# The last two heads of grouped-query attention as one written sequence, with three output groups left open

## The chip, the cores and the metric

The kernel runs on one core of one Trainium2 chip. The metric is device time in microseconds (us) of one launch; lower is better. TensorE is also called PE, VectorE DVE, ScalarE ACT, GpSimd POOL, and SyncE SP; SP issues the DMAs.

## The reference

Two layers of a trunk with two token mixers side by side. 512 latent tokens and 256 context tokens, width 1024, fp32. Each layer, for branch b (grouped-query attention, 8 query heads on 2 key heads, head width 64) and branch a (neighbourhood attention):

```python
px = hx @ w_in                                     # split into queries, keys, values, gate paths, merge gates
b_att = _gqa_latent(qb, k_all, v_all)              # softmax(q k / 8) v over 256 context + 512 latent keys
o_a = (a_att * jax.nn.silu(a_z)) @ w_o_a
o_b = (b_att * jax.nn.silu(b_z)) @ w_o_b
merged = jax.nn.sigmoid(g_a) * o_a + jax.nn.sigmoid(g_b) * o_b
x_new = x + gate_x * (merged @ w_out)
```

In layer 0 the context tokens go through the same steps (their queries read context keys only); in layer 1 only the 512 latent tokens do.

## The kernel before

Every product of fp32 values is made of reduced-precision parts: a value is split into a hi part (a cast on ACT) and a lo part (a subtraction on DVE or POOL), and a product is three matmuls (hi x hi, lo x hi, hi x lo; lines 351 to 353). A scheduler sorts the instructions of each engine by a timeline of its own; where the program calls `in_program_order` or `behind`, the written order is kept on the engines named.

Names that the text uses:

- `psf` is one PSUM bank (its pool has one buffer); `pst` are two banks for transposes; during grouped-query attention `pss` are two tiles of two banks each for scores, `psv` is one bank for values. Afterwards the last five banks are `psx`.
- For a head, `gq_scores` makes four score tiles of 128 queries x 768 keys (`pss`, L718 and L719), the row maximum (`mx`), the exp on ACT (`p`, with its row sum `r`), and `softmax_tail` scales `p` on DVE (blocks 0 and 2) or POOL (blocks 1 and 3, `GQ_POOL`). In layer 0, `ctx_scores` does the same for the context queries.
- `gq_values` goes through six blocks of 128 keys. A block is four transposes of `p` into one `pst` bank (L669), the cast to `pth` on ACT (L672), the rest `ptl` on DVE (L673), and two matmuls into `psv` (L972 with `pth`, L973 with `ptl`). `pth` and `ptl` have two buffers each. After the last block `head_out` adds the two halves of `psv` in `ho` (ACT L681, DVE L682) and multiplies the gate path `zb` with it (POOL L683). In layer 0 a seventh block (`ctx_values`, L746 and L747, 256 columns) does the context queries.
- `zb` is then split into `gbh` (ACT, L557) and `gbl` (POOL, L558), a tile row `f` for each pair of heads: the operands of the product with `w_o_b`.
- `pipeline` runs scores of head h, then values of head h - 1, then some of the `fill` pieces. In this stage these are merge-gate projections and the product of branch a with `w_o_a`: psf groups of 12 matmuls each (`psf<-gah,whi` and the like), of 512 columns and, in layer 0, also of 256 columns for the context. A group is emptied by one DVE instruction (L592, into `tg`), and the next group needs the same bank.
- After attention, `o_chunks("b", ...)` makes the product with `w_o_b`, in groups of 12 matmuls for each of eight column tiles f, with `evac_b` (L1007 to L1011) merging the two branches into `tg` and splitting the sum into `mh` and `ml`, the operands of the product with `w_out`. Weights come by DMA into `raw` and are split into `whi` (ACT, L336) and `wlo` (DVE or POOL, L338).

Of the kernel before, what the change touches and what calls it, by code (L numbers as in the profile page):

```python
# [8 lines left out]
F32 = mybir.dt.float32  # L9
F32R = mybir.dt.float32r  # L10
# [48 lines left out]
def R(ap):  # L59
    return ap.bitcast(F32R)  # L60


def F(ap):
    return ap.bitcast(F32)
# [3 lines left out]
def hybrid_kernel(es: ExitStack, tc, x, ctx, cvec, w_ada, w_ada0, small, gvec, w_in, w_o_a, w_o_b, w_out,  # L68
# [13 lines left out]
    def nm(s):  # L82
        uid[0] += 1
        return f"{s}_{uid[0]}"
# [283 lines left out]
    def chan_proj(w, f, a, n0, n1, evac):  # L368

        ps = psw(n1 - n0)  # L370
        nk = len(w)
        for k in range(nk):
            hi, lo = a(0, k), a(1, k)
            mm3(ps, (w[k][0][:, 128 * f:128 * f + 128], w[k][1][:, 128 * f:128 * f + 128]),
                (R(hi[:, n0:n1]), R(lo[:, n0:n1])), k == 0, k == nk - 1)
        evac(f, n0, n1, ps)

    hp = {"late": [], "lag": 0}

# [110 lines left out]
    def layer(l, hx, nxt, mid):  # L490
# [159 lines left out]
        if True:  # L650
# [22 lines left out]
                V.tensor_tensor(lo[:, n0:n1], pt[:, n0:n1], F(hi[:, n0:n1]), ALU.subtract)  # L673
                return hi, lo

            def head_out(po, e, dst):

                n = dst.shape[-1]
                m, o = 64 * e, 64 * (1 - e)
                t1 = att["p"].tile([128, 512], F32, tag="ho", name=nm("ho"), bufs=1)  # L680
                S.copy(t1[m:m + 64, :n], po[o:o + 64, :n])  # L681
                V.tensor_tensor(t1[m:m + 64, :n], po[m:m + 64, :n], t1[m:m + 64, :n], ALU.add)  # L682
                G.tensor_tensor(dst, dst, t1[m:m + 64, :n], ALU.mult)  # L683

            def rows(a, half):
                return a[64 * half:64 * half + 64]
# [147 lines left out]
                head_out(po, e, zv[64 * e:64 * e + 64, h // 2, 0:512])  # L834
                return vsl

            def pipeline(fill, spread, scores_of, values_of, last=None, bg=[]):

                n = len(fill)
                prev = None  # L840
                for h in range(8):
                    att["bg"] = bg if h > 3 or pm["n"] == 1 else []
                    st = scores_of(h)
# [103 lines left out]
            def gq_scores(q, kh, kl):  # L947
                ps_ = []
                for i in range(4):
                    pss = ps_score(768)  # L950
                    scores(pss, q[:, 128 * i:128 * i + 128], kh, kl,
                           [(0, 512, cut(0, 512)), (512, 256, cut(512, 768))])
                    p = p_tile()
                    mx = sp.tile([128, 2], F32, tag="mx", name=nm("mx"), bufs=8)
                    V.tensor_reduce(mx[:, 0:1], pss, AX, ALU.max, negate=True)
                    r = sp.tile([128, 2], F32, tag="r", name=nm("r"), bufs=8)
                    S.activation(p, pss, AF.Exp, bias=mx[:, 0:1], accum_out=r[:, 0:1])
                    softmax_tail(p, 768, r[:, 0:1], [(0, 768)], G if i in GQ_POOL else None)
                    ps_.append(p)
                    run(att["bg"], 1)  # L960
                return ps_
# [30 lines left out]
            pipeline(fill, 8, gq_first, values_of(zb, gq_values), early, bg)  # L992
            gq_es.close()

        with tc.tile_pool(name=f"mrg{l}", bufs=1, reuse_waits="tile") as mp:
            open_ps(x=5)
            extra = lambda name: mp.tile([128, 3072], F32, tag="extra", name=nm(name))
            gv = mp.tile([128, nv, DM], F32, tag="gate", name=nm("gate"), bufs=1)
            for v in range(nv):
                src = gd[l][8 * v:8 * v + 8].rearrange("k p -> (k p)").unsqueeze(0)  # L1000
                nc.sync.dma_start(gv[:, v, :], src.to_broadcast([128, DM]))
            hilo(zb, gated["b"], [3])
            mg = []

            def evac_b(f, n0, n1, ps):
                a, b = tg_part(0, f, n0, n1), tg_part(1, f, n0, n1)
                V.scalar_tensor_tensor(b, b, 1.0, ps, ALU.add, ALU.mult)  # L1007
                V.tensor_tensor(a, a, b, ALU.add)
                hi, lo = [m[:, f % 4, n0:n1] for m in mg[f // 4]]
                S.copy(R(hi), a)  # L1010
                V.tensor_tensor(R(lo), a, hi, ALU.subtract)  # L1011
            chunks = o_chunks("b", None, evac_b)
            chunks[0][0]()
            for i in range(4):
                if i < 3:
                    chunks[i + 1][0]()
                if i % 2 == 0:
                    mg.append(hilo_tiles("m"))
                for piece in chunks[i][1]:
                    piece()  # L1020
# [219 lines left out]
```

## Time and profile before

| | |
|---|---|
| median of 3 runs | 1148.73 us (1148.03 to 1149.26) |
| profiled execution, time | 1149.07 us |
| profiled execution, span | 1147.0 us |
| granted TensorE clock | 0.999 of full speed |
| layer 0, heads 6 and 7 | about 528 to 562 us from the span's start |
| layer 1, heads 5 to 7 | about 1054 to 1078 us |

The profile is one execution on the chip. A line of the order of time has the start, the duration, the engine, the line of the kernel, the operation with output and input tiles, and the count; in square brackets the idle time of that engine before it and what ended it. The duration of a matmul contains its latency, and matmuls overlap, so what a matmul costs is the distance from its start to the next one's.

### The profile page before, as it was taken

What the parts mean: (1) busy time and instruction counts of PE and PEld (TensorE: products, weight loads), DVE (VectorE), ACT (ScalarE), POOL (GpSimd) and SP (SyncE); (2) the same over time, 40 slices, a digit from 0 to 9 for tenths busy, and PEclk for the clock granted to TensorE, in tenths of its full rate; (3) what the DMA queues carried; (4) which work ended last, traced back from release to release, by engine and by line L of the source; (5) the groups of instructions that cost most, each with busy time, mean ns of one, the idle gap of its engine ahead of it and who ended that gap; (6) DMA issues with size and microseconds to landing.
All of it is one profiled execution on the core that took longest, in us unless ns stands there. A gap on an engine that the chain in (4) does not pass through costs nothing.

```text
span 1147.0 us, 17434 instructions
## 1 busy us (share of the span) xinstructions
PE 1123.5 (98%) x6136; PEld 949.2 (83%) x6136; DVE 818.3 (71%) x1533; ACT 580.3 (51%) x1185; POOL 483.0 (42%) x449
## 2 busy tenths in 40 slices
PE   7999999999999999999999999999999999999998
PEld 5788888888988888888788787888888888887786
DVE  6777688997454786697588755469787665898563
ACT  6553366655433565665330355336666355766421
POOL 1073355453374343453411227345554664465311
PEclk9999999999999999999999999999999999999999
DMA  9645311333322232451434424633332333152143
GB/s 370 232 127 156 90 51 60 105 110 111 106 101 89 95 103 92 92 221 38 149 127 130 151 70 122 193 89 115 97 113 74 111 102 101 65 176 90 61 133 92
DMA packets 89695, 135.08 MB, mean 118 GB/s; under 512 B 10789, under 2 KB 52745, under 8 KB 88969
## 3 DMA queue, kind: packets, MB, share of 16 engines
q1 hardware_dynamic: 89328, 133.87, 36.8%
q8 instruction: 48, 0.79, 0.3%
q14 instruction: 39, 0.31, 0.1%
q10 hardware_dynamic: 280, 0.12, 0.0%
HBM read 116.63 MB, written 17.32 MB: 117 GB/s over the span
## 4 chain that ended last, share of the span: by engine, by line
PE 80%; DVE 7%; DMA 4%; issue 3%; ACT 3%; POOL 2%; SPq 0%; POOLq 0%; ACTq 0%; DVEq 0%
PE psx L353 12%; PE psx L352 12%; PE psx L351 11%; PE psf L351 9%; PE psf L352 9%; PE psf L353 9%; PE pst L669 4%; DMA raw<-in_w_in_dram 2%; PE pss L718 2%; PE pss L719 2%; PE psv L973 2%; PE psv L972 1%; PE pss L795 1%; PE pst L431 1%; DMA rawb<-in_w_ada_dram 1%
## 5 line engine op out<-in xcount | busy, mean ns | idle before, releaser
L673 DVE TENSOR_TENSOR ptl<-pst,pth 128x512 fp32r<-128x512 f32 (+1 forms) x176 | 115.9, 671 | 46.4 <-ACT pth L672 45.4
L672 ACT CAST pth<-pst 128x512 fp32r<-128x512 f32 (+1 forms) x176 | 99.3, 577 | 86.7 <-PE pst L669 55.8
L338 POOL TENSOR_TENSOR wlo<-raw,whi 128x512 fp32r<-128x512 f32 x68 | 95.6, 1409 | 105.1 <-ACT whi L336 83.9
L351 PE MATMUL psf<-hx,whi 128*128 128x512 f32 (+1 forms) x368 | 139.2, 378 | 0.6 <-ACT zt L516 0.6
L352 PE MATMUL psf<-hx,whi 128*128 128x512 f32 (+1 forms) x368 | 138.2, 375 | 0.0
L353 PE MATMUL psf<-hx,wlo 128*128 128x512 f32 (+1 forms) x368 | 137.8, 374 | 0.0
L351 PE MATMUL psx<-whi,hx 128*128 128x512 f32 (+1 forms) x368 | 137.6, 375 | 0.0
L353 PE MATMUL psx<-whi,hx 128*128 128x512 f32 (+1 forms) x368 | 135.9, 369 | 0.1
L352 PE MATMUL psx<-wlo,hx 128*128 128x512 f32 (+1 forms) x368 | 135.7, 369 | 0.0
L336 ACT CAST whi<-raw 128x512 fp32r<-128x512 f32 x136 | 82.7, 621 | 51.6 <-DMA raw<-in_w_in_dram 35.6
L321 ACT CAST whi<-raw 128x512 fp32r<-128x512 f32 x88 | 53.9, 623 | 99.6 <-PE psx L353 38.1
L669 PE MATMUL pst<-ident,p 128*128 128x128 f32 x640 | 99.9, 272 | 1.4 <-DVE ptl L673 0.8
L324 POOL TENSOR_TENSOR wlo<-raw,whi 128x512 fp32r<-128x512 f32 x36 | 50.9, 1416 | 110.0 <-ACT whi L321 74.6
L338 DVE TENSOR_TENSOR wlo<-raw,whi 128x512 fp32r<-128x512 f32 x68 | 68.6, 1010 | 28.1 <-ACT whi L336 27.2
L669 PEld LDWEIGHTS pst<-ident,p 128*128 128x128 f32 x640 | 77.8, 140 | 13.0 <-DVE ptl L673 1.3
L658 POOL TENSOR_SCALAR r<-r 128x1 f32<-128x1 f32 x64 | 22.4, 350 | 152.2 <-DVE r L653 145.2
L659 POOL TENSOR_TENSOR p<-p,r 128x512 f32<-128x512 f32 (+1 forms) x64 | 84.2, 1316 | 5.1
L353 PEld LDWEIGHTS psx<-whi,hx 128*128 128x128 f32 x368 | 69.4, 189 | 12.6 <-DVE hx L1137 1.0
L351 PEld LDWEIGHTS psx<-whi,hx 128*128 128x128 f32 x368 | 69.5, 189 | 12.4 <-issue 0.8
L353 PEld LDWEIGHTS psf<-hx,wlo 128*128 128x128 f32 x368 | 69.4, 188 | 11.8
L351 PEld LDWEIGHTS psf<-hx,whi 128*128 128x128 f32 x368 | 69.4, 189 | 11.4 <-ACT zt L516 0.8
L352 PEld LDWEIGHTS psx<-wlo,hx 128*128 128x128 f32 x368 | 69.5, 189 | 10.8
(252 smaller groups left out, 3056.0 us busy)
## 6 DMA issues: line engine op xcount, KB each, us to landing
raw<-in_w_in_dram SPq DMA_DIRECT2D x168, 256.0 KB, 2.9
rawb<-in_w_ada_dram SPq DMA_DIRECT2D x64, 256.0 KB, 2.9
gs<-zt SPq DMA_DIRECT2D x32, 256.0 KB, 2.1
raw<-in_w_out_dram SPq DMA_DIRECT2D x32, 256.0 KB, 2.9
tg<-gs SPq DMA_DIRECT2D x4, 1536.0 KB, 6.8
rawx<-in_w_ada_dram SPq DMA_DIRECT2D x8, 512.0 KB, 7.9
raw<-in_w_o_a_dram SPq DMA_DIRECT2D x16, 256.0 KB, 2.8
raw<-in_w_o_b_dram SPq DMA_DIRECT2D x16, 256.0 KB, 2.8
```

Source lines behind the costliest of these rows:

```text
L321: S.copy(hi[:, :n], raw[:, :n])
L324: e.tensor_tensor(lo[:, :n], raw[:, :n], F(hi[:, :n]), ALU.subtract)
L336: S.copy(hi, raw)
L338: lo_eng(i).tensor_tensor(lo, raw, F(hi), ALU.subtract)
L351: T.matmul(ps, lhs[0], rhs[0], start=first, stop=False)
L352: T.matmul(ps, lhs[0], rhs[1], start=False, stop=False)
L353: T.matmul(ps, lhs[1], rhs[0], start=False, stop=last)
L659: G.tensor_tensor(p[:, c0:c1], p[:, c0:c1], r[:, i:i + 1].to_broadcast([128, c1 - c0]), ALU.mult)
L669: T.transpose(pt[:, c0:c0 + 128], src, ident)
L672: S.copy(hi[:, n0:n1], pt[:, n0:n1])
L673: V.tensor_tensor(lo[:, n0:n1], pt[:, n0:n1], F(hi[:, n0:n1]), ALU.subtract)
L718: T.matmul(ps[:, c0:c0 + n], q, sl(kh), start=True, stop=False)
```

## The change

From head 7 on, `pipeline` hands over to a `tail`: it first runs all fills that are left, then `gq_tail`. This writes the values of heads 6 and 7 as one sequence of 12 blocks (14 in layer 0, with the two context blocks in the middle), with the order on PE, ACT and DVE fixed. The transposes of a block come three blocks ahead of its matmuls; four banks (the two `pst` and one `pss` tile) and three pairs of hi and lo tiles take turns, the third pair being taken from the weight buffers `whi` and `wlo`. Head 6 collects in `psv`, head 7 in `psf`, the context blocks in the other `pss` tile. The product with `zb` moves from POOL to DVE, and so does the split of the last tile row of `zb` (`gate_part`). Behind the blocks come three column groups of the product with `w_o_b`, each with its first three of four tile rows (9 of 12 matmuls), left open; their last three matmuls follow when the last tile row is split. Their weights are loaded ahead, with the split on POOL. For head 7 the softmax scaling goes to POOL for blocks 0 and 2 in place of 1 and 3.

```diff
             def pipeline(fill, spread, scores_of, values_of, last=None, bg=[], tail=None):
...
                     st = scores_of(h)
+                    if h == 7 and tail is not None:
+                        run(fill, len(fill))
+                        last()
+                        run(bg, len(bg))
+                        return tail(prev, st)
...
-                    softmax_tail(p, 768, r[:, 0:1], [(0, 768)], G if i in GQ_POOL else None)
+                    softmax_tail(p, 768, r[:, 0:1], [(0, 768)], G if i in ((0, 2) if att["h"] == 7 else GQ_POOL) else None)
...
+            lead = [(f, 0, 512) for f in range(3)]
...
+            def gq_tail(st6, st7):
+                need_wb(0, pool_lo)
+                at = len(nc.cur_bb.bb.instructions)
+                before = next(i for i in nc.cur_bb.bb.instructions[::-1] if i.engine == ON_PE)
+                s0, s1 = psw(1024, "s"), psw(1024, "s")
+                banks = [psw(512, "t"), psw(512, "t"), s0[:, 0:512], s0[:, 512:1024]]
...
+                po6, po7 = psw(512, "v"), psw()
...
+                def turn_block(b):
+                    if b < len(blocks):
+                        pt, (hi, lo) = banks[b % 4], parts[b % 3]
+                        for src, c0 in blocks[b][0]:
+                            T.transpose(pt[:, c0:c0 + 128], src, ident)
+                        S.copy(hi, pt)
+                        V.tensor_tensor(lo, pt, F(hi), ALU.subtract)
+                for b in range(3):
+                    turn_block(b)
+                for b, (_, mm, out) in enumerate(blocks):
+                    mm(*parts[b % 3])
+                    turn_block(b + 3)
+                    if out:
+                        out()
+                    if first and b == 9:
+                        gate_part(512, 768)
+                for (f, n0, n1), ps in zip(lead, (po6, s1[:, 0:512], s1[:, 512:1024])):
+                    chan_mm(ps, wb[f // 2], f % 2, act_b, n0, n1, 0, 3)
+                    open_sums.append((f, n0, n1, ps))
+                gate_part(0, 512)
+                in_program_order((ON_PE, ON_ACT, ON_DVE), nc.cur_bb.bb.instructions[at:], {ON_PE: before.name})
+                for f, n0, n1, ps in open_sums:
+                    chan_mm(ps, wb[f // 2], f % 2, act_b, n0, n1, 3, 4)
```

How the order moves, at three places. First PE in layer 0, at the end of a psf group of the fills (`gah` and `gal` are branch a's operand, `whi` and `wlo` the weights of `w_o_a`). Before:

```order
L353 MATMUL psf_6295<-gah_5607,wlo_6067 128x256
L669 MATMUL pst_6361<-ident,p_6119 128x128
L669 MATMUL pst_6361<-ident,p_6131 128x128
L669 MATMUL pst_6361<-ident,p_6144 128x128
L669 MATMUL pst_6361<-ident,p_6156 128x128
L746 MATMUL psv_6258<-pth_6254,vb_3532 128x256
L747 MATMUL psv_6258<-ptl_6255,vb_3532 128x256
```

Now, at the end of such a group:

```order
L351 MATMUL psf_6206<-gah_5607,whi_6065 128x256
L352 MATMUL psf_6206<-gal_5608,whi_6065 128x256
L353 MATMUL psf_6206<-gah_5607,wlo_6067 128x256
L351 MATMUL psf_6220<-gah_5607,whi_6059 128x512
L352 MATMUL psf_6220<-gal_5608,whi_6059 128x512
L353 MATMUL psf_6220<-gah_5607,wlo_6061 128x512
```

The transposes and value matmuls of heads 6 and 7 stood between the groups; now six groups (512, 256, 512, 256, 512, 256 columns) follow one another without anything in between, and the sequence of heads 6 and 7 starts behind the last of them.

Second, DVE in layer 0, from head 6's context output to head 7's two outputs (before), and from the end of head 6 through the two context blocks (now). `tg` with `psf` is the emptying of a fill's group, `wlo<-raw` a weight split. Before:

```order
L682 TENSOR_TENSOR ho_6263<-psv_6258,ho_6263 64x256
L592 SCALAR_TENSOR_TENSOR tg_5619<-tg_5619,psf_6309 128x512
L673 TENSOR_TENSOR ptl_6378<-pst_6372,pth_6377 128x512
L673 TENSOR_TENSOR ptl_6389<-pst_6383,pth_6388 128x512
L592 SCALAR_TENSOR_TENSOR tg_5619<-tg_5619,psf_6323 128x256
L338 TENSOR_TENSOR wlo_6636<-raw_6632,whi_6634 128x512
L673 TENSOR_TENSOR ptl_6400<-pst_6394,pth_6399 128x512
L673 TENSOR_TENSOR ptl_6411<-pst_6405,pth_6410 128x512
L673 TENSOR_TENSOR ptl_6426<-pst_6420,pth_6425 128x512
L682 TENSOR_TENSOR ho_6416<-psv_6349,ho_6416 64x512
L682 TENSOR_TENSOR ho_6434<-psv_6429,ho_6434 64x256
```

Now:

```order
L1069 TENSOR_TENSOR wlo_6293<-pst_6286,whi_6292 128x512
L685 TENSOR_TENSOR ho_6362<-psv_6294,ho_6362 64x512
L686 TENSOR_TENSOR zb_4186<-zb_4186,ho_6362 64x512
L1069 TENSOR_TENSOR ptl_6289<-pst_6287,pth_6288 128x512
L685 TENSOR_TENSOR zt_6376<-pss_6285,zt_6376 64x256
L686 TENSOR_TENSOR zb_4186<-zb_4186,zt_6376 64x256
L1069 TENSOR_TENSOR ptl_6291<-pss_6284,pth_6290 128x512
L685 TENSOR_TENSOR zt_6390<-pss_6285,zt_6390 64x256
L686 TENSOR_TENSOR zb_4186<-zb_4186,zt_6390 64x256
L1069 TENSOR_TENSOR wlo_6293<-pss_6284,whi_6292 128x512
L1069 TENSOR_TENSOR ptl_6289<-pst_6286,pth_6288 128x512
L1055 TENSOR_TENSOR gbl_6253<-zb_4186,gbh_6252 128x256
```

The products `zb<-zb,ho` and `zb<-zb,zt` and the split `gbl` now stand in DVE's queue between the splits of the blocks, and no fill's `tg` does.

Third, ACT in layer 1, behind the output of head 5 (`ho_11571` before, `ho_11536` now). Before:

```order
L681 COPY ho_11571<-psv_11504 64x512
L672 CAST pth_11685<-pst_11680 128x512
L672 CAST pth_11696<-pst_11691 128x512
L557 CAST gbh_11785<-zb_10309 128x512
L672 CAST pth_11707<-pst_11702 128x512
L672 CAST pth_11718<-pst_11713 128x512
L672 CAST pth_11729<-pst_11724 128x512
```

Now:

```order
L684 COPY ho_11536<-psv_11469 64x512
L1068 CAST pth_11717<-pst_11714 128x512
L1068 CAST whi_11719<-pss_11711 128x512
L336 CAST whi_11892<-raw_11890 128x512
L336 CAST whi_11898<-raw_11896 128x512
L336 CAST whi_11921<-raw_11919 128x512
L559 CAST gbh_11679<-zb_10274 128x512
L1068 CAST pth_11715<-pss_11711 128x512
```

Three weight casts (`whi<-raw`, for later groups of `w_o_b`) and the cast of a tile row of `zb` stand between the casts of the third and the fourth block.

More of the change, by code (lines that the diff above doesn't have):

```diff
@@ L370, in chan_proj, with chan_mm @@
         ps = psw(n1 - n0)
-        nk = len(w)
-        for k in range(nk):
+        chan_mm(ps, w, f, a, n0, n1, 0, len(w))
+        evac(f, n0, n1, ps)
+    def chan_mm(ps, w, f, a, n0, n1, k0, k1):
+        for k in range(k0, k1):
             hi, lo = a(0, k), a(1, k)
             mm3(ps, (w[k][0][:, 128 * f:128 * f + 128], w[k][1][:, 128 * f:128 * f + 128]),
-                (R(hi[:, n0:n1]), R(lo[:, n0:n1])), k == 0, k == nk - 1)
-        evac(f, n0, n1, ps)
+                (R(hi[:, n0:n1]), R(lo[:, n0:n1])), k == 0, k == len(w) - 1)
     hp = {"late": [], "lag": 0}
@@ L835, in na_values, with pipeline @@
                 return vsl
-            def pipeline(fill, spread, scores_of, values_of, last=None, bg=[]):
+            def pipeline(fill, spread, scores_of, values_of, last=None, bg=[], tail=None):
                 n = len(fill)
@@ L991, in layer, with need_wb @@
             bg = gate_steps((1,), att["p"]) if first else []
-            pipeline(fill, 8, gq_first, values_of(zb, gq_values), early, bg)
+            wb = {}
+            def need_wb(f, lo=mix_lo):
+                for i in range(f // 2, min(f // 2 + 2, 4)):
+                    if i not in wb:
+                        wb[i] = load_w2(w_o_b[l], 256 * i, 4, lo)
+            act_b = lambda part, k: gated["b"][part][:, k, :]
+            groups = [(f, n0, n1) for f in range(8) for n0, n1 in spans]
@@ new lines, in layer, with evac_b @@
+            pipeline(fill, 8, gq_first, values_of(zb, gq_values), early, bg, gq_tail)
+            mg = []
+            def evac_b(f, n0, n1, ps):
+                a, b = tg_part(0, f, n0, n1), tg_part(1, f, n0, n1)
+                V.scalar_tensor_tensor(b, b, 1.0, ps, ALU.add, ALU.mult)
+                V.tensor_tensor(a, a, b, ALU.add)
+                if f // 4 == len(mg):
+                    mg.append(hilo_tiles("m"))
+                hi, lo = [m[:, f % 4, n0:n1] for m in mg[f // 4]]
+                S.copy(R(hi), a)
+                V.tensor_tensor(R(lo), a, hi, ALU.subtract)
@@ L993, in layer @@
+            for f, n0, n1, ps in open_sums:
+                evac_b(f, n0, n1, ps)
             gq_es.close()
@@ L1001, in layer @@
                 nc.sync.dma_start(gv[:, v, :], src.to_broadcast([128, DM]))
[L1002 to L1020, printed above, removed]
+            for f, n0, n1 in groups:
+                if (f, n0, n1) not in lead:
+                    need_wb(f)
+                    chan_proj(wb[f // 2], f % 2, act_b, n0, n1, lambda _, a, b, ps, f=f: evac_b(f, a, b, ps))
             nt = 6 if first else 4
```

45 lines of the change are left out of this document (42 added, 3 removed).

## The prediction, made before the changed kernel ran

> **What bounds the kernel now.** I read the page first (busy shares, chain), then the order of time around the end of both grouped-query attentions (about 528 to 562 us in layer 0, 1050 to 1080 us in layer 1), matmul by matmul.
>
> ```profile
> PE 1123.5 (98%) x6136; PEld 949.2 (83%) x6136; DVE 818.3 (71%) x1533; ACT 580.3 (51%) x1185; POOL 483.0 (42%) x449
> ```
>
> TensorE is busy 98% of the span, so only two things move the end: matmuls removed (none are: the same transposes and matmuls are issued) and TensorE's short waits. Each wait must therefore be found by the distance between matmul starts. The following rows of the order of time (start, duration, engine, line) give the distances, and show how layer 0 hides the emptying of its one psf bank.
>
> ```profile
> 500.80 0.69 DVE L592 SCALAR_TENSOR_TENSOR tg<-tg,psf 128x512 f32<-128x512 f32 x1
> ...
> 501.54 0.39 PE L351 MATMUL psf<-gah,whi 128*128 128x256 f32 x1 [0.66 <-DVE tg L592]
> ...
> 542.28 0.39 PE L353 MATMUL psf<-gah,wlo 128*128 128x512 f32 x1
> ...
> 542.71 0.69 DVE L592 SCALAR_TENSOR_TENSOR tg<-tg,psf 128x512 f32<-128x512 f32 x1 [1.39 <-PE psf L353]
> ...
> 544.24 0.36 PE L351 MATMUL psf<-gah,whi 128*128 128x256 f32 x1
> ...
> 546.68 0.60 PE L669 MATMUL pst<-ident,p 128*128 128x128 f32 x4
> ...
> 547.03 0.47 PE L351 MATMUL psf<-gah,whi 128*128 128x512 f32 x1
> ...
> 547.34 0.39 PE L352 MATMUL psf<-gal,whi 128*128 128x512 f32 x1
> ...
> 547.57 0.39 PE L353 MATMUL psf<-gah,wlo 128*128 128x512 f32 x1
> ...
> 552.54 0.28 PE L353 MATMUL psf<-gah,wlo 128*128 128x256 f32 x1
> ...
> 552.86 0.42 DVE L592 SCALAR_TENSOR_TENSOR tg<-tg,psf 128x256 f32<-128x256 f32 x1 [0.22 <-PE psf L353]
> ```
>
> Unhindered, 512 columns cost 0.23 us (547.34 to 547.57), 256 columns half of it, 0.12, and four transposes with what they add to the next matmul 0.44 (547.34 minus 546.68, less 0.23, rounded). One block of values (four transposes, hi and lo matmul) is then 0.90 us.
>
> A psf group's bank is free again 0.43 + 0.69 us after its last matmul starts (542.28, 542.71), and the next group starts 0.05 us later (501.49 to 501.54): 1.17 us, 0.94 more than the matmul's own 0.23. After a 256-column group it is 0.32 + 0.42 + 0.05 - 0.12 = 0.67 us. At 542.28 to 544.24 that is hidden, because transposes and value matmuls stand between the two groups. At 501.54, with DVE behind, it shows. Layer 0's real losses today are two, behind the fills:
>
> ```profile
> 557.53 0.40 PE L351 MATMUL psf<-gbh,whi 128*128 128x512 f32 x1
> ...
> 558.71 0.50 PE L352 MATMUL psf<-gbl,whi 128*128 128x512 f32 x1 [0.78 <-POOL gbl L558]
> ...
> 560.70 0.28 PE L353 MATMUL psx<-gbh,wlo 128*128 128x256 f32 x1
> ...
> 562.18 0.50 PE L351 MATMUL psx<-gbh,whi 128*128 128x512 f32 x1 [1.20 <-DVE ho L682]
> ```
>
> These are 1.18 - 0.23 = 0.95 and 1.48 - 0.12 = 1.36, together 2.3 us. Layer 1 has half as many fills, and its last heads lie bare:
>
> ```profile
> 1053.77 0.39 PE L353 MATMUL psf<-gah,wlo 128*128 128x512 f32 x1
> ...
> 1056.29 1.75 DVE L338 TENSOR_TENSOR wlo<-raw,whi 128x512 fp32r<-128x512 f32 x1
> ...
> 1058.69 0.50 PE L973 MATMUL psv<-ptl,vb 128*128 128x512 f32 x1 [1.54 <-DVE ptl L673]
> ...
> 1075.78 0.60 PE L669 MATMUL pst<-ident,p 128*128 128x128 f32 x4
> ...
> 1076.42 0.59 ACT L672 CAST pth<-pst 128x512 fp32r<-128x512 f32 x1 [0.55 <-PE pst L669]
> ...
> 1077.04 0.69 DVE L673 TENSOR_TENSOR ptl<-pst,pth 128x512 fp32r<-128x512 f32 x1 [0.44 <-ACT pth L672]
> ...
> 1077.78 0.50 PE L973 MATMUL psv<-ptl,vb 128*128 128x512 f32 x1 [0.22 <-DVE ptl L673]
> ...
> 1078.12 0.40 PE L351 MATMUL psx<-gbh,whi 128*128 128x512 f32 x1
> ```
>
> From the last fill matmul (1053.77) to the first psx matmul (1078.12) are 24.35 us. In them lie 16 sets of four transposes, 36 value matmuls, 9 matmuls of psf<-gbh and four score matmuls (two of 512, two of 256 columns): 16 x 0.44 + 45 x 0.23 + 0.7 = 18.1. Lost: 6.2 us. From the transposes' start to the lo matmul a block takes 2.00 us (1075.78 to 1077.78), so a lead of one block (0.90 us) can't cover it; a lead of three (2.24 us of other PE work up to hi) can, as long as ACT and DVE keep pace.
>
> **The change, part by part.** *Layer 0, fills in a row.* Heads 6 and 7 leave the fills. Six psf groups (512, 256, 512, 256, 512, 256 columns) now stand one behind the other on one bank. Five handovers are bare. Four cost 2 x 0.94 + 2 x 0.67 = 3.2 us. The first is dearer: DVE has to finish the context softmax of head 7 and head 5's output first, and ACT casts gbh before that softmax:
>
> ```profile
> 531.69 1.57 ACT L557 CAST gbh<-zb 128x768 fp32r<-128x768 f32 x2
> ...
> 534.50 0.43 DVE L682 TENSOR_TENSOR ho<-psv,ho 64x256 f32<-64x256 f32 x1
> ...
> 534.63 0.47 ACT L735 ACTIVATE p<-pss,mx 128x256 f32<-128x256 f32 x1
> ...
> 536.01 0.61 DVE L656 TENSOR_SCALAR p<-p,r 128x256 f32<-128x256 f32 x2
> ```
>
> ACT reaches gbh at about 531.1 (one pth cast fewer ahead of it), is through two exps at 531.1 + 1.57 + 2 x 0.47 + 0.2 = 533.8; DVE then needs 0.2 + 0.61 + 0.43 + 0.69 = 1.9, to 535.7. The group itself ends by 533.9 (before: 532.30 start; now 1.1 earlier, without three sets of transposes but with a short wait for scores). Cost 1.9 us, bounds 0.94 and 2.5.
>
> The Trainium skill's Perfetto Trace Analysis, section Matmuls, says the same against this order: independent groups should rotate through PSUM banks, so that one's evacuation lies beside the next group's matmuls. If all five handovers were hidden as it asks, the sum below would be 5.1 us smaller. The rows at 542.28 and 501.54 agree with it.
>
> *Layer 0, the sequence of 14 blocks.* PE needs 14 x 0.90 = 12.6 us. DVE has more to do, since the products zb move to it from POOL and a weight split (wlo<-raw) and gbl fall between the blocks. No row shows zb on DVE; the nearest is another product of two SBUF tiles:
>
> ```profile
> 569.72 0.42 DVE L1008 TENSOR_TENSOR tg<-tg,tg 128x256 f32<-128x256 f32 x1
> ...
> 1086.51 1.78 DVE L1008 TENSOR_TENSOR tg<-tg,tg 128x512 f32<-128x512 f32 x1
> ...
> 1088.81 0.68 DVE L1008 TENSOR_TENSOR tg<-tg,tg 128x512 f32<-128x512 f32 x1
> ```
>
> Sum on DVE: 14 x 0.69 + wlo 1.75 (1056.29, POOL at work too, as here) + ho 0.69 + 2 x 0.43 + zb 0.68 + 2 x 0.42 + gbl 0.42 = 14.9. I take the short value for zb since POOL has no work by then, and both ends for the range. The first lo starts 1.25 us after the first transposes; DVE waits some 0.4 for ACT, which stands three raw casts (0.62 each) between block 2 and block 3; the last lo matmul ends 0.3 later: 16.8 us, 4.2 lost. Bounds 2.5 (every split 0.64, wlo 0.69) and 5.5 (zb 1.78).
>
> The Trainium skill's SBUF — State Buffer, section Who interferes with whom, says a DVE instruction with two SBUF inputs and a GpSimd one that reads SBUF exclude each other for the whole instruction. By it wlo would be 0.69 plus a POOL split of about 1.3, 2.0 in place of 1.75, and the sum 0.2 larger; 1056.29 is near that.
>
> Today's 2.3 us go: gbl is done long before, and 27 matmuls of the open sums (27 x 0.23 = 6.2 us) cover the last output (ho, ho, zb, gbh, gbl: about 0.6 + 3 x 0.69 + 0.62 + latencies = 3.5 us, 5 with a weight split ahead). Layer 0: 3.2 + 1.9 + 4.2 - 2.3 = **+7.0 us**.
>
> *Layer 1.* No fills pile up there. Rows for the outputs and casts:
>
> ```profile
> 1053.93 0.62 ACT L336 CAST whi<-raw 128x512 fp32r<-128x512 f32 x1
> ...
> 1066.15 0.62 ACT L557 CAST gbh<-zb 128x512 fp32r<-128x512 f32 x1 [0.30 <-POOL zb L683]
> ...
> 1070.97 0.58 ACT L681 COPY ho<-psv 64x512 f32<-64x512 f32 x1
> ...
> 1071.66 0.68 DVE L682 TENSOR_TENSOR ho<-psv,ho 64x512 f32<-64x512 f32 x1
> ...
> 1072.42 1.29 POOL L683 TENSOR_TENSOR zb<-zb,ho 64x512 f32<-64x512 f32 x1 [4.29 <-DVE ho L682]
> ```
>
> Head 5's last four blocks keep the lead of one and lose what stands between them now: I work out 0.4 + 0.05 + 0.35 + 0.85 = 1.6 us, the last because ACT does head 7's fourth exp, and DVE its scaling, ahead of the split. In the sequence, ACT does ho (0.58), two block casts (1.18), three raw casts (1.86) and gbh (0.62) before block 3's cast (0.59) and DVE's 0.69: ready 5.6 us after head 5's last matmul, where PE comes to it at 3.8. Loss 1.75 (bounds 0.5 and 3). Block 1 behind ho loses 0.25, and ho and zb of head 6 on DVE push blocks 9 to 11 back by 1.1. Sum 4.7 against 6.2 now: **-1.5 us**. Between, the 1.54 us wait at 1058.69 goes, since these weight splits are on POOL.
>
> SP's queue keeps its order but for one DMA of w_out past the xt loads, whose weights are wanted over 10 us later: nothing.
>
> Sum: +7.0 - 1.5 = +5.5 us. The profiled execution took 1149.07 us, 1147.0 of it span; it lies 0.34 above the median 1148.73. Forecast: 1154.6 for such an execution, 1154.2 for the median.
>
> **Rivals.** *The lead hides both sequences* (not slower). If DVE's extras find room beside PE, as they would if DVE's share per block stayed below 0.90, layer 0 keeps only bare handovers (3 x 0.94 + 2 x 0.67 = 4.2, plus 0.4 at the start, less 2.3: +2.3) and layer 1 only 1.4 of its 6.2 (-4.8): -2.5, 1146.2. For it: DVE needs 0.69 a block alone. Against: 14.9 over 12.6. It decides from extras under some 3 us per sequence.
>
> *Small on both sides:* low bounds in layer 0 (3.2 + 0.94 + 2.5 - 2.3 = +4.3), and 3 lost in layer 1 (-3.2): +1.1, 1149.8.
>
> *ACT and DVE fall behind in both:* the raw casts delay block 3, and the queue never recovers; layer 0 at 2.5 + 5.5 (+8.9), layer 1 at 7.7 (+1.5): 1159. For it: both queues are in written order, so one late cast holds all.
>
> *The clock falls.* The waits and the many transposes might let the granted clock drop; at half of it the 12.6 us of layer 0's sequence would cost 12.6 more: 1167.
>
> ```profile
> 1050.00:1060.00 10.00, 8.46 (x48) 6.84 (x47) 8.57 (x13) 6.19 (x13) 6.83 (x6) 1.00 0.17 51
> 1070.00:1080.00 10.00, 9.28 (x46) 6.39 (x45) 5.74 (x9) 4.68 (x8) 1.53 (x2) 1.00 0.16 52
> ```
>
> These stretches have waits up to 1.54 us and as many transposes, at a granted clock of 1.00 (third number from the right). The Trainium skill's TensorE: Matmul & The Clock Gate, Part 4, says transposes don't count as activity for the gate; no wait so far has cost clock here.
>
> **How the numbers follow.** A measurement of this kernel can tell about 0.2%, 2.3 us. Forecast 0.58; lead hides both 0.14; small 0.13; both behind 0.12; clock 0.03. Of the second, around -2.5, 0.10 is faster and 0.04 the same; the small one is the same; of the forecast's own spread 0.02 falls within 2.3 us. So faster 0.10, same 0.19, slower 0.71. The forecast's own range is 1151 to 1158; the range for 8 in 10 takes in the small case and reaches to the rival behind: 1148.8 to 1159.
>
> **What would show it.** Right: waits of PE psf on DVE tg in layer 0, five of about 0.7 to 2 us at 530 to 550 us; then DVE without idle time through the sequence and lo matmuls waiting for ptl; no wait on gbl or ho ahead of psx. In layer 1 one wait of 1 to 2 us at the fourth block. Wrong: no psf waits (something else is between the groups), or DVE idle during the sequences, or zb on DVE near 1.8 us.

## The result, and the profile after

| | before | after |
|---|---|---|
| median of 4 runs each | 1148.81 us (1148.03 to 1149.26) | 1160.09 us (1159.89 to 1160.51) |
| span of the profiled execution | 1147.0 us | 1158.4 us |

The ratio of the times is 1.0100, with a 95% interval of 1.0087 to 1.0113: 11.3 us slower. Slower was forecast, but by half of that, and the time lies outside the range.

First the page and the view of waits of the changed kernel (engine, what waits, its line, the releaser; us in total, times, longest):

```profile
PE 1125.9 (97%) x6136; PEld 950.7 (82%) x6136; DVE 820.6 (71%) x1538; ACT 580.4 (50%) x1186; POOL 479.7 (41%) x445
...
PE psf L351 <- DVE tg L594: 4.8, 6, 1.5
...
PE pss L1067 <- DVE ptl L1069: 4.2, 4, 1.8
...
PE pss L1043 <- DVE zt L685: 2.9, 1, 2.9
...
PE pss L1067 <- DVE wlo L1069: 1.3, 2, 0.7
```

TensorE does the same 6136 instructions. Five of the six waits in the first row are the handovers of the psf bank, which the prediction had; the sixth, 0.7 us at about 501 us, was there before. The other three are waits of instructions that write a `pss` tile: six sets of transposes (L1067), and one context matmul (L1043), 8.4 us together. The prediction had none of these. It expected TensorE to wait at the lo matmuls, for their operand.

Which layer lost the time? Up to head 7 the order on PE is the same in both kernels, and both issue the same number of matmuls from a score matmul just ahead of the changed part to the first matmul of `w_out` (`psx<-whi,mh`). In layer 0, before:

```profile
526.59 0.48 PE L718 MATMUL pss<-gk,qs 128*128 128x512 f32 x1
...
592.62 0.40 PE L351 MATMUL psx<-whi,mh 128*128 128x512 f32 x1
```

After:

```profile
527.02 0.48 PE L721 MATMUL pss<-gk,qs 128*128 128x512 f32 x1
...
604.42 0.40 PE L351 MATMUL psx<-whi,mh 128*128 128x512 f32 x1
```

That is 66.0 us before and 77.4 after: layer 0 accounts for 11.4 us, as much as the spans differ. In layer 1 such a distance is 72.1 us before (1025.76 to 1097.88) and 72.4 after (1036.85 to 1109.24). Below, lost time is the distance between matmul starts less the nominal costs of the prediction.

The handovers came as forecast. In order of time:

```profile
534.39 0.39 PE L353 MATMUL psf<-gah,wlo 128*128 128x512 f32 x1
...
535.10 0.43 DVE L685 TENSOR_TENSOR ho<-psv,ho 64x256 f32<-64x256 f32 x1
535.56 0.69 DVE L594 SCALAR_TENSOR_TENSOR tg<-tg,psf 128x512 f32<-128x512 f32 x1
...
536.30 0.39 PE L351 MATMUL psf<-gah,whi 128*128 128x256 f32 x1 [1.52 <-DVE tg L594]
```

The first costs 1.91 - 0.23 = 1.68 us, the four behind it 0.67, 0.94, 0.67 and 0.94: 4.9 us in all, where 5.1 were forecast.

The sequence in layer 0 lost 8.5 us instead of 4.2: from its first transpose to the first matmul of `w_o_b` (549.92 to 571.04) are 21.1 us, where 14 blocks need 12.6. Its waits, with what DVE and ACT did ahead of each:

```profile
552.44 0.68 DVE L1069 TENSOR_TENSOR wlo<-pss,whi 128x512 fp32r<-128x512 f32 x1
...
553.17 0.66 PE L1067 MATMUL pss<-ident,p 128*128 128x128 f32 x4 [0.70 <-DVE wlo L1069]
...
557.19 0.69 DVE L1069 TENSOR_TENSOR ptl<-pss,pth 128x512 fp32r<-128x512 f32 x1 [0.15 <-ACT pth L1068]
557.94 0.65 PE L1067 MATMUL pss<-ident,p 128*128 128x128 f32 x4 [0.93 <-DVE ptl L1069]
...
559.25 0.69 DVE L1069 TENSOR_TENSOR ptl<-pss,pth 128x512 fp32r<-128x512 f32 x1 [1.36 <-ACT pth L1068]
...
559.81 0.60 PE L1067 MATMUL pst<-ident,p 128*128 128x128 f32 x4
...
560.88 0.68 DVE L685 TENSOR_TENSOR ho<-psv,ho 64x512 f32<-64x512 f32 x1
561.60 0.68 DVE L686 TENSOR_TENSOR zb<-zb,ho 64x512 f32<-64x512 f32 x1
562.21 0.68 DVE L1069 TENSOR_TENSOR ptl<-pst,pth 128x512 fp32r<-128x512 f32 x1
562.81 0.41 DVE L685 TENSOR_TENSOR zt<-pss,zt 64x256 f32<-64x256 f32 x1
...
563.27 0.58 PE L1043 MATMUL pss<-pth,vb 128*128 128x256 f32 x1 [2.86 <-DVE zt L685]
...
566.00 0.69 DVE L1069 TENSOR_TENSOR ptl<-pss,pth 128x512 fp32r<-128x512 f32 x1 [2.34 <-ACT pth L1068]
```

Count the blocks from 0. Block 2 is transposed into the first half of a `pss` tile, block 3 into the second half, another bank. Yet block 3's transposes start at 553.17, just when DVE has read block 2 out of the first half (552.44 + 0.68). Block 7 waits for block 6 in the same way at 557.94, and block 11 for block 10 later (a wait of 0.55 us at 566.75). Blocks 2, 6 and 10, which go into the first half, and the blocks in the two `pst` banks show no such wait. At 563.27 the second context block, which collects in the second half of the other `pss` tile, waits until DVE has emptied the first context block's sum from the first half (`zt`), and that stands in DVE's queue behind `ho`, `zb` and a split. So at every fourth block the lead of three blocks is gone: the transposes wait for a split that is one block old. And DVE, which was to be the bound, stands idle itself for 1.36 and 2.34 us (ahead of 559.25 and 566.00), because TensorE, waiting for it, gives it nothing.

The time behind that wait is dear too. Stretches of the same execution (length; busy time of PE, PEld, DVE, ACT, POOL; then the granted clock, DMA share and GB/s):

```profile
559.90:563.20 3.30, 0.51 (x5) 0.27 (x3) 3.00 (x6) 1.81 (x4) 0.00 (x0) 1.00 0.20 69
563.20:566.70 3.50, 2.93 (x10) 2.21 (x10) 1.12 (x3) 0.95 (x2) 0.00 (x0) 0.51 0.00 0
566.70:571.00 4.30, 4.05 (x22) 3.09 (x23) 3.52 (x7) 2.58 (x5) 0.00 (x0) 1.00 0.00 0
```

After 2.86 us without work TensorE ran at a granted clock of 0.51 for 3.5 us. With 2.93 us busy in it, that is some 1.4 us (an estimate: half of the busy time); the 8.5 us contain it.

Layer 1 shows the same pattern three times:

```profile
1073.36 0.50 PE L1031 MATMUL psv<-pth,vb 128*128 128x512 f32 x1 [0.58 <-DVE ho L685]
...
1074.68 0.66 PE L1067 MATMUL pss<-ident,p 128*128 128x128 f32 x4 [0.59 <-DVE wlo L1069]
...
1079.45 0.66 PE L1067 MATMUL pss<-ident,p 128*128 128x128 f32 x4 [0.94 <-DVE ptl L1069]
...
1085.06 0.66 PE L1067 MATMUL pss<-ident,p 128*128 128x128 f32 x4 [1.76 <-DVE ptl L1069]
```

The wait for `psv` (0.58) is the release of head 5's bank; the three others are blocks 3, 7 and 11.

### The profile page after: what moved, and what is told of

It reads as the page before. It is cut to its first block, busy times and chain, and to the rows that moved or that the text cites. A ratio compares the mean times of both kernels' runs of the same rounds, so it can differ in the third digit from the quotient of the medians.

```text
span 1158.4 us, 17433 instructions
## 1 busy us (share of the span) xinstructions
PE 1125.9 (97%) x6136; PEld 950.7 (82%) x6136; DVE 820.6 (71%) x1538; ACT 580.4 (50%) x1186; POOL 479.7 (41%) x445
## 4 chain that ended last, share of the span: by engine, by line
PE 84%; DVE 6%; DMA 3%; issue 2%; ACT 2%; POOL 2%; SPq 0%; ACTq 0%; POOLq 0%; DVEq 0%
PE psx L353 11%; PE psx L351 11%; PE psx L352 11%; PE psf L351 10%; PE psf L352 9%; PE psf L353 9%; PE pst L671 4%; PE pss L721 2%; PE pss L722 2%; PE pss L798 1%; PE psv L982 1%; PE pst L433 1%; PE psv L981 1%; DMA raw<-in_w_in_dram 1%; DMA rawb<-in_w_ada_dram 1%
## 5 line engine op out<-in xcount | busy, mean ns | idle before, releaser
L338 POOL TENSOR_TENSOR wlo<-raw,whi 128x512 fp32r<-128x512 f32 x72 | 101.1, 1409 | 100.8 <-ACT whi L336 69.0
L351 PE MATMUL psx<-whi,hx 128*128 128x512 f32 (+1 forms) x376 | 140.8, 376 | 0.0
L353 PE MATMUL psx<-whi,hx 128*128 128x512 f32 (+1 forms) x376 | 139.2, 370 | 0.0
L352 PE MATMUL psx<-wlo,hx 128*128 128x512 f32 (+1 forms) x376 | 138.7, 369 | 0.0
L675 DVE TENSOR_TENSOR ptl<-pst,pth 128x512 fp32r<-128x512 f32 (+1 forms) x150 | 98.6, 669 | 38.3 <-ACT pth L674 37.4
L674 ACT CAST pth<-pst 128x512 fp32r<-128x512 f32 (+1 forms) x150 | 84.3, 575 | 75.0 <-PE pst L671 49.8
L324 POOL TENSOR_TENSOR wlo<-raw,whi 128x512 fp32r<-128x512 f32 x36 | 52.1, 1448 | 143.6 <-ACT whi L321 87.3
L671 PE MATMUL pst<-ident,p 128*128 128x128 f32 x536 | 84.2, 272 | 0.6 <-DVE r L655 0.6
L338 DVE TENSOR_TENSOR wlo<-raw,whi 128x512 fp32r<-128x512 f32 x64 | 61.2, 957 | 29.1 <-ACT whi L336 28.4
L353 PEld LDWEIGHTS psx<-whi,hx 128*128 128x128 f32 x376 | 70.9, 189 | 12.9 <-DVE hx L1230 0.8
L351 PEld LDWEIGHTS psx<-whi,hx 128*128 128x128 f32 x376 | 71.0, 189 | 12.6 <-issue 0.8
L351 PEld LDWEIGHTS psf<-hx,whi 128*128 128x128 f32 x368 | 69.4, 189 | 10.8 <-ACT zt L518 0.2
L352 PEld LDWEIGHTS psf<-hx,whi 128*128 128x128 f32 x368 | 69.4, 189 | 10.5
```

The costliest lines, as they stand in the source:

```text
L324: e.tensor_tensor(lo[:, :n], raw[:, :n], F(hi[:, :n]), ALU.subtract)
L338: lo_eng(i).tensor_tensor(lo, raw, F(hi), ALU.subtract)
L351: T.matmul(ps, lhs[0], rhs[0], start=first, stop=False)
L352: T.matmul(ps, lhs[0], rhs[1], start=False, stop=False)
L353: T.matmul(ps, lhs[1], rhs[0], start=False, stop=last)
L671: T.transpose(pt[:, c0:c0 + 128], src, ident)
```

## The experiments

Two theories. **A**: the halves of one `pss` tile are one thing to the waits, so that a write into one half waits for the reader of the other. **B**, the prediction's: DVE's sum of work sets the pace, and where TensorE happens to wait is no matter. Each ratio is against the kernel before, run beside it.

| edit, from the changed kernel | median, us | ratio, 95% interval |
|---|---|---|
| sequence in layer 1 alone | 1149.17 | 1.0006 (0.9997 to 1.0015) |
| banks in another order | 1157.81 | 1.0078 (1.0065 to 1.0090) |
| context output later | 1157.33 | 1.0075 (1.0063 to 1.0088) |
| zb back on POOL | 1158.58 | 1.0086 (1.0072 to 1.0100) |
| banks and context output | 1155.12 | 1.0060 (1.0047 to 1.0073) |
| these, and fills between the blocks | 1151.68 | 1.0026 (1.0016 to 1.0037) |
| these, and head 6's zb on POOL | 1150.83 | 1.0021 (1.0012 to 1.0030) |
| layer 1 alone, banks, fills, zb | 1147.05 | 0.9988 (0.9979 to 0.9997) |
| layer 1 alone, banks, zb, head 6 in psf | 1146.26 | 0.9978 (0.9970 to 0.9987) |
| the same, and layer 0 with fills and outputs apart | 1147.51 | 0.9987 (0.9978 to 0.9996) |
| layer 1 alone, banks, zb, head 6 in psf, late weight casts | 1145.33 | 0.9972 (0.9962 to 0.9983) |

Two parts of the change were not run alone: the softmax scaling of head 7 on POOL for other blocks, and the three groups left open.

**Which layer.** In layer 0 the softmax scaling of head 7 and the split of the last tile row also go back to what they were (not shown in the cut):

```diff
-            lead = [(f, 0, 512) for f in range(3)]
+            lead = [] if first else [(f, 0, 512) for f in range(3)]
...
-            pipeline(fill, 8, gq_first, values_of(zb, gq_values), early, bg, gq_tail)
+            pipeline(fill, 8, gq_first, values_of(zb, gq_values), early, bg, None if first else gq_tail)
```

> The sequence in layer 1 alone; layer 0 is left as in the kernel before. Reading of the changed kernel's trace (layer 0 lost 10.8 us more than before, layer 1 lost 9.3 instead of 9.4): 1148.7 us, no change against before. By the prediction's own terms (layer 1 gains 1.5): 1147.2. If the cost had come from layer 1: 1155 or more.

1149.17 us, no change that can be told from the kernel before. Layer 0 costs the 11 us, and layer 1 brings nothing, as the distances said. The prediction's gain of 1.5 in layer 1 isn't there.

**The order of the banks.**

```diff
-                banks = [psw(512, "t"), psw(512, "t"), s0[:, 0:512], s0[:, 512:1024]]
+                t0, t1 = psw(512, "t"), psw(512, "t")
+                banks = [t0, s0[:, 0:512], t1, s0[:, 512:1024]]
```

> The four banks take turns in another order: pst, first half of the pss tile, pst, second half. Theory A (the two halves of one pss tile are one thing to the waits, so that a block's transposes into the second half wait for the lo split of the block just before, in the first half): the waits of 0.70, 0.93 and 0.55 us in layer 0 and of 0.59, 0.94 and 1.76 in layer 1 go, about 0.96 + 1.10 + 0.95 + 0.76 + 1.10 + 1.93 = 6.7 us of lost time with them, and 1 to 2 come back as waits for a split: 1155 us. Theory B (the prediction's: DVE's sum of 14.9 us sets the pace of the sequence): the order of the banks is no matter, 1160 within 1 us, and the waits move to the lo matmuls.

1157.81 us, 2.3 faster. The same work with the two halves used two blocks apart; its view of waits:

```profile
PE pss L1044 <- DVE zt L685: 2.6, 1, 2.6
...
PE pss L1068 <- DVE ptl L1070: 1.3, 2, 0.9
...
PE pss L1068 <- DVE wlo L1070: 0.2, 1, 0.2
```

The six waits of transposes, 5.5 us, are down to three of 1.5 us in all. Nothing else was changed, DVE's sum least of all, so these waits were for the other half of the tile. The gain is smaller than the 5 us expected: waits for the splits themselves come up, of 0.2 to 0.9 us, and in layer 1 the wait for head 5's `ho` grew from 0.58 to 1.18.

**The context output.**

```diff
+                    if first and b == 7:
+                        blocks[6][2]()
-                    if out:
+                    if out and not (first and b == 6):
                         out()
```

> In layer 0 the output of head 6's context block (copy, addition, product) is issued behind the matmuls of head 7's context block in place of ahead of them. Theory A (both collect in halves of one pss tile, and the second's first matmul waits for the first's reader): the wait of 2.86 us at 563.27 goes, 1157 us. Theory B (DVE is behind by then in any case): the time comes back as waits for ptl on the next blocks, 1160 within 1 us.

1157.33 us, 2.8 faster. The wait on `zt` is gone, and so is the slow clock:

```profile
563.20:566.70 3.50, 3.32 (x20) 2.73 (x21) 3.37 (x9) 2.60 (x6) 0.00 (x0) 1.00 0.00 0
```

Part of it comes back in the row that was at 4.2 us:

```profile
PE pss L1067 <- DVE ptl L1069: 5.4, 4, 1.8
```

TensorE reaches block 11 earlier and waits 1.77 us there, for block 10's split in the other half.

**The product zb on POOL.**

```diff
-  head_out(po, e, zv[64 * e:64 * e + 64, 3, 0:512], None, V)
+  head_out(po, e, zv[64 * e:64 * e + 64, 3, 0:512])
...
-  head_out(po, e, zv[64 * e:64 * e + 64, 3, 512:768], t1, V)
+  head_out(po, e, zv[64 * e:64 * e + 64, 3, 512:768], t1)
```

> The products zb of heads 6 and 7 go back to POOL; all else as changed. Theory B (DVE's sum sets the pace): 0.68 + 2 x 0.42 us less on DVE in layer 0's sequence and 0.68 in layer 1's, 2 us faster, 1158. Theory A (the waits are on shared tiles): DVE has idle time in the sequence anyway; only the wait of 1.76 us in layer 1, behind ho and zb, shortens by up to 0.6: 1159.5 to 1160.

1158.58 us, 1.5 faster, between the theories: DVE's load counts as well, since the releasing instruction stands behind it in DVE's queue. The trace shows where: two waits, the one for `zt` and the one of block 11 in layer 1, are 0.72 us shorter each (2.86 to 2.14, 1.76 to 1.04). The median hides a spread of 1157.45 to 1159.85, and the profiled execution, the slowest, shows a part of the reason:

```profile
559.40:562.00 2.60, 0.50 (x5) 0.26 (x3) 2.32 (x5) 1.80 (x4) 0.87 (x1) 1.00 0.21 76
562.00:563.60 1.60, 1.56 (x10) 1.21 (x10) 0.00 (x0) 0.35 (x1) 1.08 (x2) 0.96 0.00 0
563.60:570.20 6.60, 5.73 (x20) 4.72 (x20) 3.18 (x6) 3.04 (x7) 0.73 (x1) 0.50 0.00 0
570.20:572.00 1.80, 1.80 (x9) 1.41 (x8) 1.18 (x3) 0.72 (x2) 0.00 (x0) 0.97 0.05 14
```

The wait for `zt` was shorter, but the clock was at half for 6.6 us instead of 3.5.

**Both at once** (banks in turn and the late context output).

> Both edits at once: the banks in the order pst, half, pst, half, and head 6's context output behind head 7's context matmuls. Theory A (shared tiles): more than the sum of the two, since the wait of 1.77 us that appeared at block 11 with the late context output alone is again one half of a tile waiting for the other: 1160.1 - 2.3 - 2.8 - 1.5 = 1153.5; TensorE's clock stays at 1.00. Theory B (DVE's sum): at most the sum, 1155, and waits for ptl and wlo at the lo matmuls.

1155.12 us, 5.0 faster than the changed kernel, which is the plain sum of the two edits and not more; A's 1153.5 was not reached. By its time alone this run doesn't tell the theories apart. What is left of the waits of transposes:

```profile
PE pss L1068 <- DVE ptl L1070: 2.2, 3, 0.9
...
PE pss L1068 <- DVE wlo L1070: 1.0, 1, 1.0
```

Each of these four now waits for a split two blocks old, which the matmuls just behind need as well: this is DVE's lag, and to this extent B holds. Layer 0's sequence loses 4.9 us in this kernel. Layer 1, counted as the prediction did from the last fill matmul to the first of `w_o_b`, loses 5.7 (1060.38 to 1082.07, 21.7 us, less 16.0) where the changed kernel loses 7.5 (1063.89 to 1087.45, 23.6 us).

**The fills between the blocks.** The last chunk of fills (four groups in layer 0, two in layer 1) is kept for the sequence, and head 7 takes psf only behind them:

```diff
-                        run(fill, len(fill))
+                        run(fill, len(fill) - 2 * len(spans))
...
                 for b, (_, mm, out) in enumerate(blocks):
+                    run(fill, 1)
+                    if not fill and not po7:
+                        po7.append(psw())
                     mm(*parts[b % 3])
```

> Both edits, and the last chunk of fills (four psf groups in layer 0, two in layer 1) stands between the first blocks of the sequence instead of ahead of it; head 7 takes psf behind the last of them. If the handovers of the one psf bank cost what their rows say (0.67 + 0.94 + 0.67 + 0.94 = 3.2 us), and the first group hides the start of the sequence (0.9 in layer 0, 1.4 in layer 1): 1153.5 - 5.5 = 1148. If only the handovers matter: 1150. If DVE, which has to empty the groups among the splits, falls behind: 1153 or more.

1151.68 us, 3.4 faster than without. The row of the handovers, 4.8 us in six, becomes

```profile
PE psf L351 <- DVE tg L594: 2.1, 2, 1.5
```

so 2.7 us of bare handovers and the start of the sequence are hidden. Less than the 5.5 hoped for, and about what the handovers alone were to bring (3.2): in layer 1 the same two groups had covered head 5, which now loses 4.1 us at its blocks where it lost 1.4 without the edit, and in layer 0 the lag behind `ho`, `zb` and two `zt` shows as a wait of 1.79 us.

**And head 6's zb on POOL.**

```diff
-  head_out(po6 if h == 6 else po7[0], e, zv[64 * e:64 * e + 64, 3, 0:512], None, V)
+  head_out(po6 if h == 6 else po7[0], e, zv[64 * e:64 * e + 64, 3, 0:512], None, G if h == 6 else V)
```

> As the one before, and the product zb of head 6 on POOL in place of DVE. By the wait at block 11 in layer 1 (0.92 us left with the banks in turn, behind ho and zb on DVE): 0.6 us less, 1147.4. If that wait is not DVE's: no change, 1148.

1150.83 us, 0.85 faster; the two intervals overlap, so the times alone don't settle it. In the trace block 11 of layer 1 loses 0.36 us instead of 1.08, about as expected. In layer 0 a wait of 2.06 us (559.94) has taken the place of those of 1.79 and 1.00, with a lower clock behind it.

**Layer 1 alone, with these.** The edit of the first experiment together with the banks in turn, the fills between the blocks and head 6's zb on POOL.

> The sequence in layer 1 alone, with the banks in turn, its last two fills between its first blocks and head 6's zb on POOL; layer 0 as in the kernel before. Layer 1 lost 9.4 us before and would lose about 5: 1148.6 - 4 = 1144.5. If the waits come back elsewhere: 1147 to 1149.

1147.05 us: faster than the kernel before for the first time, by 1.5 us instead of 4, as the second expectation has it. The waits of the sequence itself come to 1.2 us, but the others came back at head 5's blocks, where the two groups of fills had stood.

**Head 6 in psf** (fills ahead again, the two banks that collect the heads exchanged), in layer 1 alone, with the banks in turn and head 6's zb on POOL.

```diff
-                po6, po7 = psw(512, "v"), psw()
+                po7, po6 = psw(512, "v"), psw()
```

> The sequence in layer 1 alone, banks in turn, head 6's zb on POOL, fills ahead of the sequence as in the changed kernel (where they cover head 5), and head 6 collects in psf, head 7 in psv, so that the first block needs not wait for head 5's output (1.44 us with the banks in turn). If each wait goes by its row, layer 1 loses 9.4 - 5.5: 1148.6 - 5.5 = 1143. If what is taken away turns up as waits of head 5's last blocks, as with the fills moved: 1147.

1146.26 us, 2.7 faster than the kernel before; half of what the rows promised. The wait for `ho` is gone, and behind it the fourth block now shows what the prediction had warned of. Its split (1064.24) stands behind weight casts and a weight split, and the transposes of the sixth block, which write the other half of its tile, wait for it:

```profile
1061.99 1.66 ACT L336 CAST whi<-raw 128x512 fp32r<-128x512 f32 x3
...
1063.16 1.15 DVE L338 TENSOR_TENSOR wlo<-raw,whi 128x512 fp32r<-128x512 f32 x1
1064.24 0.68 DVE L1070 TENSOR_TENSOR ptl<-pss,pth 128x512 fp32r<-128x512 f32 x1
...
1064.97 0.66 PE L1068 MATMUL pss<-ident,p 128*128 128x128 f32 x4 [1.29 <-DVE ptl L1070]
```

**The sequence in layer 0 too**, with its last four fills between the first blocks, the two context outputs behind blocks 7 and 9, and their products on POOL.

```diff
-                        run(fill, len(fill))
+                        run(fill, len(fill) - (2 * len(spans) if first else 0))
...
-                    if out:
+                    if first and b in (7, 9):
+                        blocks[6 if b == 7 else 7][2]()
+                    if out and not (first and b in (6, 7)):
                         out()
-                    if first and b == 9:
+                    if first and b == 11:
                         gate_part(512, 768)
```

> The same in layer 1, and the sequence in layer 0 too: the last four fills between its first blocks, the two context outputs two and three blocks behind their matmuls and apart, their products and head 6's on POOL. Layer 0 lost 2.3 us around the heads before and keeps the first handover and head 7's scores (1.66 + 0.47) and the start of the last blocks (0.8): the same as the one before within 1 us. If the DVE lag at the end of layer 0's sequence (1.95 + 1.16 us with the fills moved) stays: 3 us more than the one before.

1147.51 us, 1.25 more than the one before. From the same score matmul to the first matmul of `w_out`, layer 0 takes 67.0 us here (527.75 to 594.80) and 66.0 there (526.84 to 592.88): 1.0 us more, most of the difference. Even without the waits the written order is no better in layer 0 than fills between the heads, since the first handover (1.68 us) stays bare.

**Late weight casts**, from the kernel with head 6 in psf: the weights of the later groups are loaded right behind the sequence, their casts and splits kept behind it on ACT and DVE.

```diff
-                in_program_order((ON_PE, ON_ACT, ON_DVE), nc.cur_bb.bb.instructions[at:], {ON_PE: before.name})
+                done = in_program_order((ON_PE, ON_ACT, ON_DVE), nc.cur_bb.bb.instructions[at:], {ON_PE: before.name})
+                at = len(nc.cur_bb.bb.instructions)
+                need_wb(4)
+                in_program_order((ON_ACT, ON_DVE), nc.cur_bb.bb.instructions[at:], done)
```

> As the one with head 6 in psf, and the weight casts and splits that the scheduler had put between the third and the fourth block of layer 1 (three casts on ACT, 1.66 us, one split on DVE, 1.15) are kept behind the sequence. The prediction's term for layer 1 (1.75 us lost behind these casts): the wait of 1.29 us at the fourth block's transposes goes: 1146.3 - 1.4 = 1144.9. If that wait is head 5's output and split on DVE: no change, 1146.3. If the late weights are missed by the groups of w_o_b behind: 1147 or more.

1145.33 us, 3.5 us (0.28%, 0.17 to 0.38) faster than the kernel before and the fastest of all. The gain over the kernel with head 6 in psf, 0.9 us, is not settled by the times, since the two intervals overlap and the two kernels ran on different chips. The traces do show it: from the same score matmul to the first of `w_out`, layer 1 takes 68.6 us (1024.91 to 1093.47) and took 69.8 (1025.69 to 1095.53). The wait of 1.29 us is gone; one of 0.2 is left:

```profile
PE pss L1068 <- DVE ptl L1070: 0.2, 1, 0.2
```

## Why the prediction was right on the sign and wrong on the size

- **The six fills in a row**: 5.1 us forecast, 4.9 measured. Right, the first one included (1.9 forecast, 1.68 measured; head 7's scores lost another 0.46 us behind ACT).
- **Today's 2.3 us of layer 0**: gone, as forecast.
- **The 14 blocks of layer 0**, 4.2 us with bounds of 2.5 and 5.5: this is the step that failed, with 8.5 measured. It held DVE's sum against TensorE's and took the lead of three blocks for granted, "as long as ACT and DVE keep pace"; I did not ask what each transpose has to wait for. The four banks are two tiles of one bank and one tile of two, and a write into one half waits for the reader of the other. That, and the context block that waited in the same way, brought 0.96, 1.10, 3.11 and 0.95 us, and the slower clock behind the longest of them some 1.4. With both waits taken away, the sequence loses 4.9 us and the whole kernel takes 1155.1, near the forecast of 1154.2. It could have been asked beforehand: the list of `banks` in the change has the two halves of `s0` next to each other.
- **Within that sum**, zb on DVE took 0.68 us, the end that I chose. The weight split took 1.06 us and not 1.75. And the sum took each DVE instruction at its duration, 0.69, where DVE instructions that wait for nothing start 0.60 us apart (561.60, 562.21, 562.81). So DVE's own work was smaller than the 14.9 worked out; that the time with the shared halves parted comes near the forecast is in part luck.
- **Layer 1**, 4.7 us forecast in place of 6.2: 7.5 by the same count. Head 5's last blocks lost 1.7 (1.6 forecast). The waits of blocks 3, 7 and 11 (0.76, 1.10, 1.93 with their followers) took the place of the terms for the weight casts (1.75) and for ho and zb (1.1). With the banks in turn the count is 5.7. The term of the weight casts was hidden behind the earlier waits and showed as 1.45 us only when these were gone.
- **The clock.** I gave 0.03 to a clock that falls, and argued that no wait so far had cost clock. The longest wait in those stretches was 1.54 us; the new one was 2.86, and it did: about 1.4 us, not the 12.6 that the rival asked for. This rival was true in a small dose, and it fed on the wait that I had not seen.
- **The rival that both fall behind** gave 1159, near the result, but by late casts that hold the queue. The casts between block 2 and 3 held nothing in layer 0. It was right by its time and wrong in its mechanism.
- **Signs asked for**: psf waits, five of 0.7 to 2 us, and no wait on `gbl` or `ho` ahead of the last groups: seen. DVE without idle time, and lo matmuls that wait: wrong, DVE idled, and the transposes waited. One wait of 1 to 2 us at the fourth block of layer 1: it was 0.59, and for the half tile.

## What to carry to other kernels

When buffers take turns, list for each write the last reader of everything that shares its tile, not only of its own bytes; in this kernel a tile of two banks counted as one buffer, and neighbours in the turn should not share it. A lead of n blocks is worth what the oldest of these readers leaves of it. And before moving filler work ahead of a sequence, ask what it covers where it stands: here it was worth 5 us in layer 0 and 2.7 at head 5 in layer 1 (4.1 less 1.4).

## What the runs showed of the hardware

In these traces each wait of TensorE of 2 to 3 us was followed by half its clock, for a time that differs from trace to trace: 0.51 for 3.5 us after a wait of 2.86 us, 0.50 for 6.6 us after one of 2.14 us, and there the first 1.6 us behind the wait still ran at 0.96. After a wait of 1.77 us (with the late context output, the row of 563.20) it stayed at 1.00, after one of 2.62 us (banks in another order) it was 0.57 from 562.00 to 566.00, and after one of 2.06 us (fills, and head 6's zb on POOL) it fell as well:

```profile
560.00:563.30 3.30, 3.30 (x11) 2.72 (x12) 2.15 (x4) 1.11 (x2) 0.00 (x0) 0.52 0.01 2
```

The five runs of the kernel with the banks in another order took 1155.9 us at a mean clock of 0.999, 1157.4 to 1158.2 at 0.997, and 1158.9 at 0.995: the time of one program goes with its clock over 3 us, where the kernel with the late context output, which has no such wait, spreads by 0.7. The clock is not the only cause of spread: the kernel of layer 1 alone with fills between the blocks spreads by 2.7 us (1146.51 to 1149.24) at clocks of 0.999 and 1.000.

The Trainium skill's TensorE: Matmul & The Clock Gate, section Why this matters for your kernels, asks for no gaps over some 3 us. The trace says less: waits of 2.06 to 2.86 us were enough here. But transposes stand at the edges of these waits; from the start of one matmul that is no transpose to that of the next are 2.86 (with zb on POOL), 3.10 and 3.58 us where the clock fell, and at most 2.60 where it did not, and the runs don't tell which of the two counts. Part 1 of the same page of the Trainium skill has a window of about 3.4 us that runs freely. The rows above give 3.4 us at half clock in the changed kernel ((1 - 0.51) x 3.5 / 0.5) and in the same way 6.8 with zb on POOL, which is one and two of these, though no run here shows the window itself.

A DVE split of two SBUF tiles took 1.06 us (553.25) and 1.15 us (1063.16 above) beside POOL's work, and 0.68 at 570.56, where POOL had none:

```profile
553.25 1.06 DVE L338 TENSOR_TENSOR wlo<-raw,whi 128x512 fp32r<-128x512 f32 x1
...
550.14 5.87 POOL L560 TENSOR_TENSOR gbl<-zb,gbh 128x768 fp32r<-128x768 f32 x3 [13.75 <-PE psf L353]
```

POOL was at work from 550.14 to 556.01 without a break, so the neighbour cost 0.38 us here. It does not always cost: in the trace of the changed kernel all 54 weight splits on DVE without POOL's work beside them took about 0.7 us; of the 22 with it all along, 10 took 0.7 and 12 took 1.1 to 2.0. The prediction took 1.75 for this split, from a row of the kernel before, and worked out 2.0 from the Trainium skill's SBUF — State Buffer, section Who interferes with whom, by which such a pair excludes each other for the whole instruction. Neither size came up in this sequence.
